# Column sums of an 8192 x 8192 matrix: two rows per partition and load, fp32 sums on TensorE in four column tiles, and a last block in narrowing strips

## The chip, the cores and the metric

The kernel runs on one core of one Trainium2 chip. The metric is the device time of one execution in microseconds (us), lower is better. Profiles show one execution; their span, from the first instruction to the last, is about 1.8 us shorter than the timed figure. "Fast" and "slow" are states of an execution.

## The reference

```python
def setup_inputs():
    return {"x": np.random.randn(8192, 8192).astype(np.float32)}   # seeded

def reference(x):
    return np.sum(x, axis=0)
```

The input is 268.4 MB, the output 32 KB. Every input byte is read once and there is almost no arithmetic per byte.

## The kernel before

It walks over 64 blocks of 128 rows. Each block is a load of 4 MB (a partition gets one row of 32 KB). ScalarE and VectorE cast it to bf16 in four slices, and TensorE sums over the partitions with a column of ones: 16 matmuls of 512 columns. The sums of the left half of the columns stay in PSUM partition 0, those of the right half in partition 64. After the last block two single-partition copies bring them to SBUF, and two stores send them out.

```python
    load_pool = ctx.enter_context(tc.tile_pool(name="loads", bufs=4))
    bf_pool = ctx.enter_context(tc.tile_pool(name="bf", bufs=3))
    ...
    for i in range(n_row_blocks):                      # 64 blocks of 128 rows
        xt = load_pool.tile([P, C], mybir.dt.float32)
        xb = bf_pool.tile([P, C], mybir.dt.bfloat16)
        nc.sync.dma_start(out=xt, in_=xr[i])           # 4 MB
        for s in range(nsplit):                        # 4 casts of 2048 columns
            eng = nc.scalar if s % 2 == 0 else nc.vector
            ...                                        # copy / tensor_copy
        for g in range(n_col_groups):                  # 16 matmuls of 512 columns
            ...                                        # opart = 0 or 64
            nc.tensor.matmul(out=psum[opart:opart + 1, off:off + N], lhsT=ones,
                             rhs=xb[:, g * N:(g + 1) * N],
                             start=(i == 0), stop=(i == n_row_blocks - 1))

    nc.vector.tensor_copy(out=res[0:1, :], in_=psum[0:1, :])
    nc.scalar.copy(out=res[64:65, :], in_=psum[64:65, :])
    nc.sync.dma_start(out=out[0:HALF], in_=res[0:1, :])
    nc.sync.dma_start(out=out[HALF:C], in_=res[64:65, :])
```

## Time and profile before

| | before |
|---|---|
| timed median (three runs; a fourth, below, makes it 646.06) | 645.85 us |
| profiled span | 644.0 us |
| first load landed / last load landed | 13.1 / 626.9 us |
| tail: last landing to the end | 17.1 us |

These are lines of the page of the kernel before: the span, the busy time of each engine with its share of the span, the DMA share (tenths) in 40 slices, the load queue's share of 16 DMA engines, the queue of instruction fetches (packets, MB, share), and the chain of waits that ended last.

```profile
span 644.0 us, 2724 instructions
PE 336.7 (52%) x1024; PEld 97.4 (15%) x1024; DVE 155.6 (24%) x129; ACT 241.6 (38%) x130; POOL 0.3 (0%) x5
DMA  9999999999999999999999999999999999999970
...
q1 hardware_dynamic: 9220, 268.47, 97.0%
q8 instruction: 8, 0.13, 0.1%
...
DMA 88%; ACT 5%; issue 4%; PE 1%; DVE 1%; SPq 0%; ACTq 0%
```

The loads bound the kernel: the 16 DMA engines are busy until the last slice but one, no compute engine is busy for more than about half the span, and the chain is 88% load. To see how fast loads come, look at when VectorE, which waits for each, starts its casts. The next fence is the timeline of VectorE: start, duration, engine, line, operation, count, and in brackets the idle time before it and what ended it.

```profile
568.60 2.36 DVE L52 CAST xb<-xt 128x2048 bf16<-128x2048 f32 x2 [7.35 <-DMA xt<-in_x_dram]
578.31 2.36 DVE L52 CAST xb<-xt 128x2048 bf16<-128x2048 f32 x2 [7.34 <-DMA xt<-in_x_dram]
588.03 2.36 DVE L52 CAST xb<-xt 128x2048 bf16<-128x2048 f32 x2 [7.36 <-DMA xt<-in_x_dram]
```

A 4 MB load lands every 9.71 to 9.72 us, 431.7 GB/s. The end of the chain of waits (start, duration, what) shows the tail, everything after the last landing:

```profile
591.73 35.03 DMA xt<-in_x_dram
626.86 1.91 ACT xb L50
628.81 4.50 PE psum L60 x15
633.34 4.42 DVE res L69
637.78 3.56 ACT res L70
```

A cast, fifteen matmuls, then two PSUM copies that run one after the other although they are on different engines, and 2.7 us of store and end up to 644.0.

### The profile page before, as it was taken

Reading aid. Unit: us, or ns where it says so; the run is one execution under the profiler, and the core shown is the slowest. Engines: PE = TensorE matmul, PEld = TensorE weight load, DVE = VectorE, ACT = ScalarE, POOL = GpSimd, SP = SyncE. Lnnn points to the kernel's source line nnn. Section 1 sums busy time; section 2 is a strip of 40 time slices with the busy share of each in tenths; the row PEclk is TensorE's granted clock in tenths of the full one; section 3 lists DMA queues with packets and bytes.
Section 4 is the critical chain, followed back from the end, with each engine's and each line's share of the span. In section 5 each row is a group of like instructions: output and inputs, shape, how many; then the busy total and the mean of one; then the engine's idle time right before and its main releaser. Section 6 shows DMA issues by size and latency. Waiting matters only on the chain.

```text
span 644.0 us, 2724 instructions
## 1 busy us (share of the span) xinstructions
PE 336.7 (52%) x1024; PEld 97.4 (15%) x1024; DVE 155.6 (24%) x129; ACT 241.6 (38%) x130; POOL 0.3 (0%) x5
## 2 busy tenths in 40 slices
PE   1464653655545644654646546635555547446533
PEld 0111111111111111111111111101111111111110
DVE  1122122222221221221221221221221221222223
ACT  2243243342442442442442432433433433433423
POOL 0000000000000000000000000000000000000000
PEclk9767668667767687678676766676678676876686
DMA  9999999999999999999999999999999999999970
GB/s 387 427 423 440 435 427 423 444 432 426 426 440 434 422 429 442 429 425 433 438 429 427 434 431 432 429 436 434 426 429 430 438 427 430 429 438 429 434 339 2
DMA packets 9233, 268.64 MB, mean 417 GB/s; under 512 B 1026, under 2 KB 1026, under 8 KB 1026
## 3 DMA queue, kind: packets, MB, share of 16 engines
q1 hardware_dynamic: 9220, 268.47, 97.0%
q8 instruction: 8, 0.13, 0.1%
q14 instruction: 5, 0.04, 0.0%
HBM read 268.44 MB, written 0.03 MB: 417 GB/s over the span
## 4 chain that ended last, share of the span: by engine, by line
DMA 88%; ACT 5%; issue 4%; PE 1%; DVE 1%; SPq 0%; ACTq 0%
DMA xt<-in_x_dram 88%; ACT xb L50 5%; PE psum L60 1%; DVE res L69 1%; ACT res L70 1%; SPq L46 0%; ACTq L50 0%
## 5 line engine op out<-in xcount | busy, mean ns | idle before, releaser
L60 PE MATMUL psum<-xb,ones 128*1 128x512 bf16 x1024 | 336.7, 570 | 296.6 <-DVE xb L52 290.7
L50 ACT CAST xb<-xt 128x2048 bf16<-128x2048 f32 x128 | 236.7, 1896 | 391.8 <-DMA xt<-in_x_dram 391.8
L52 DVE CAST xb<-xt 128x2048 bf16<-128x2048 f32 x128 | 151.2, 1224 | 478.0 <-DMA xt<-in_x_dram 478.0
L60 PEld LDWEIGHTS <-ones 128*1 128x1 bf16 x1024 | 97.4, 107 | 535.3 <-issue 521.9
L70 ACT COPY res<-psum 1x4096 f32<-1x4096 f32 x1 | 3.6, 3564 | 7.2 <-DVE res L69 7.2
L69 DVE COPY res<-psum 1x4096 f32<-1x4096 f32 x1 | 4.4, 4411 | 4.1 <-PE psum L60 4.1
L50 ACT ACT_TABLE_LOAD x1 | 1.3, 1283 | 0.7 <-PEq L87 0.7
L37 POOL MEMSET ones<- 128x1 bf16 x1 | 0.1, 102 | 0.3 <-POOLq L87 0.3
L87 POOL MEMSET const-bfloat16-1.0<- 128x1 bf16 x1 | 0.1, 102 | 0.0
L87 POOL MEMSET const-uint8-127<- 128x1 uint8 x1 | 0.1, 102 | 0.0
L87 POOL MEMSET const-float32-0.0<- 128x1 f32 x1 | 0.1, 99 | 0.2 <-issue 0.2
L87 POOL MEMSET const-float32-1.0<- 128x1 f32 x1 | 0.1, 99 | 0.0
## 6 DMA issues: line engine op xcount, KB each, us to landing
xt<-in_x_dram SPq DMA_DIRECT2D x64, 4096.0 KB, 35.0
out_dram<-res SPq DMA_DIRECT2D x2, 16.0 KB
```

The costliest lines, as they stand in the source:

```text
L37: nc.gpsimd.memset(ones, 1.0)
L50: eng.copy(out=xb[:, s * CS:(s + 1) * CS], in_=xt[:, s * CS:(s + 1) * CS])
L52: eng.tensor_copy(out=xb[:, s * CS:(s + 1) * CS], in_=xt[:, s * CS:(s + 1) * CS])
L60: nc.tensor.matmul(out=psum[opart : opart + 1, off : off + N], lhsT=ones, rhs=xb[:, g * N : (g + 1) * N], start=(i == 0), stop=(i == n_row ...
L69: nc.vector.tensor_copy(out=res[0:1, :], in_=psum[0:1, :])
L70: nc.scalar.copy(out=res[64:65, :], in_=psum[64:65, :])
L87: nc = _bacc.Bacc("TRN2", target_bir_lowering=False, num_devices=1)
```

## The change

The intent is to feed the DMA engines larger pieces, to take both casts away (VectorE adds two rows in fp32, TensorE sums in fp32, four matmuls side by side in column tiles of 32), and to shorten the tail: the last block comes in strips of 8, 4, 2, 1 and 1 units of 512 columns, and each strip's sums are copied and stored as soon as they are complete.

```diff
-    xr = x.rearrange("(b p) c -> b p c", p=P)
+    xr = x.rearrange("(b p k) c -> b p k c", p=P, k=K)          # K = 2
-    load_pool = ctx.enter_context(tc.tile_pool(name="loads", bufs=4))
-    bf_pool = ...
+    load_pool = ctx.enter_context(tc.tile_pool(name="loads", bufs=3))
-    ones = const_pool.tile([P, 1], mybir.dt.bfloat16)
+    ones = const_pool.tile([P, 32], F32)
...                                   # casts and bf16 matmuls go
+    for t in range(n_blocks - 1):
+        xt = load_pool.tile([P, K, C], F32, tag="xt")
+        nc.sync.dma_start(out=xt, in_=xr[t])                      # 8 MB
+        for b in range(n_banks):                                  # 4 banks
+            cols = slice(b * BANK, (b + 1) * BANK)                # BANK = 2048
+            nc.vector.tensor_tensor(out=xt[:, 0, cols], in0=xt[:, 0, cols],
+                                    in1=xt[:, 1, cols], op=mybir.AluOpType.add)
+            v = xt[:, 0, cols].rearrange("p (q j i) -> p j q i", q=NQ, j=NJ)
+            for j in range(NJ):              # out=psum[32*j:32*j+32, ...]
+                mm(v[:, j], j, 512 * b, 512, t == 0, False)
...
+    for u0, nu in STRIPS:                    # [(0,8),(8,4),(12,2),(14,1),(15,1)]
+        cols = slice(u0 * 512, (u0 + nu) * 512)
+        nc.sync.dma_start(out=last[:, :, cols], in_=xr[t][:, :, cols])
+    for u0, nu in STRIPS:
...     # add on VectorE where nu >= 4, else both rows go to TensorE; matmuls into psum
+        nc.vector.tensor_copy(out=res[:, 128*u0 : 128*(u0+nu)],
+                              in_=psum[:, 128*u0 : 128*(u0+nu)])
+        nc.sync.dma_start(out=outr[:, u0:u0+nu, :], in_=res[0:97:32, ...])
```

More of the change, by code (lines that the diff above doesn't have):

```diff
@@ L7 @@
 from concourse._compat import with_exitstack
+F32 = mybir.dt.float32
+BANK = 2048
+NQ, NJ, NI = 4, 4, 128
+STRIPS = [(0, 8), (8, 4), (12, 2), (14, 1), (15, 1)]
 @with_exitstack
@@ L19 @@
     R, C = x.shape
-    assert R % P == 0
-    n_row_blocks = R // P
-    N = 512
-    assert C % N == 0
-    n_col_groups = C // N
-    HALF = C // 2
-    xr = x.rearrange("(b p) c -> b p c", p=P)
-    const_pool = ctx.enter_context(tc.tile_pool(name="const", bufs=1))
-    load_pool = ctx.enter_context(tc.tile_pool(name="loads", bufs=4))
-    bf_pool = ctx.enter_context(tc.tile_pool(name="bf", bufs=3))
-    psum_pool = ctx.enter_context(tc.tile_pool(name="psum", bufs=1, space=bass.MemoryType.PSUM))
@@ L34 @@
-    out_pool = ctx.enter_context(tc.tile_pool(name="out", bufs=1))
-    ones = const_pool.tile([P, 1], mybir.dt.bfloat16)
-    nc.gpsimd.memset(ones, 1.0)
-    psum = psum_pool.tile([P, HALF], mybir.dt.float32)
-    nsplit = 4
-    CS = C // nsplit
-    for i in range(n_row_blocks):
-        xt = load_pool.tile([P, C], mybir.dt.float32)
-        xb = bf_pool.tile([P, C], mybir.dt.bfloat16)
-        nc.sync.dma_start(out=xt, in_=xr[i])
-        for s in range(nsplit):
-            eng = nc.scalar if s % 2 == 0 else nc.vector
-            if eng is nc.scalar:
-                eng.copy(out=xb[:, s * CS:(s + 1) * CS], in_=xt[:, s * CS:(s + 1) * CS])
-            else:
-                eng.tensor_copy(out=xb[:, s * CS:(s + 1) * CS], in_=xt[:, s * CS:(s + 1) * CS])
-        for g in range(n_col_groups):
-            if g < n_col_groups // 2:
-                opart = 0
-                off = g * N
-            else:
-                opart = 64
-                off = (g - n_col_groups // 2) * N
-            nc.tensor.matmul(
-                out=psum[opart : opart + 1, off : off + N],
-                lhsT=ones,
-                rhs=xb[:, g * N : (g + 1) * N],
-                start=(i == 0),
-                stop=(i == n_row_blocks - 1),
-            )
@@ L68 @@
-    res = out_pool.tile([P, HALF], mybir.dt.float32)
-    nc.vector.tensor_copy(out=res[0:1, :], in_=psum[0:1, :])
-    nc.scalar.copy(out=res[64:65, :], in_=psum[64:65, :])
-    nc.sync.dma_start(out=out[0:HALF], in_=res[0:1, :])
-    nc.sync.dma_start(out=out[HALF:C], in_=res[64:65, :])
+    K = 2
+    assert R % (P * K) == 0 and C % BANK == 0
+    n_blocks = R // (P * K)
+    n_banks = C // BANK
+    xr = x.rearrange("(b p k) c -> b p k c", p=P, k=K)
+    outr = out.rearrange("(u j i) -> j u i", j=NJ, i=NI)
@@ new lines @@
+    const_pool = ctx.enter_context(tc.tile_pool(name="const", bufs=1))
+    load_pool = ctx.enter_context(tc.tile_pool(name="loads", bufs=3))
+    psum_pool = ctx.enter_context(
+        tc.tile_pool(name="psum", bufs=1, space=bass.MemoryType.PSUM)
+    )
+    res_pool = ctx.enter_context(tc.tile_pool(name="res", bufs=1))
+    ones = const_pool.tile([P, 32], F32)
+    nc.gpsimd.memset(ones, 1.0)
+    psum = psum_pool.tile([P, n_banks * 512], F32)
+    res = res_pool.tile([P, n_banks * 512], F32)
@@ new lines, in mm @@
+    def mm(rhs, j, lo, n, start, stop):
+        nc.tensor.matmul(
+            out=psum[32 * j : 32 * j + 32, lo : lo + n],
+            lhsT=ones,
+            rhs=rhs,
+            start=start,
+            stop=stop,
+            skip_group_check=True,
+        )
+    for t in range(n_blocks - 1):
[3 more added lines that the diff above has]
+            cols = slice(b * BANK, (b + 1) * BANK)
+            nc.vector.tensor_tensor(
+                out=xt[:, 0, cols], in0=xt[:, 0, cols], in1=xt[:, 1, cols],
+                op=mybir.AluOpType.add,
+            )
+            v = xt[:, 0, cols].rearrange("p (q j i) -> p j q i", q=NQ, j=NJ)
+            for j in range(NJ):
+                mm(v[:, j], j, 512 * b, 512, t == 0, False)
@@ new lines @@
+    t = n_blocks - 1
+    last = load_pool.tile([P, K, C], F32, tag="xt")
+    for u0, nu in STRIPS:
+        cols = slice(u0 * 512, (u0 + nu) * 512)
+        nc.sync.dma_start(out=last[:, :, cols], in_=xr[t][:, :, cols])
+    for u0, nu in STRIPS:
+        cols = slice(u0 * 512, (u0 + nu) * 512)
+        for w in range(u0, u0 + nu, 4):
+            m = min(4, u0 + nu - w)
+            rows = [0, 1]
+            if nu >= 4:
+                wc = slice(w * 512, (w + m) * 512)
+                nc.vector.tensor_tensor(
+                    out=last[:, 0, wc], in0=last[:, 0, wc], in1=last[:, 1, wc],
+                    op=mybir.AluOpType.add,
+                )
+                rows = [0]
+            for k in rows:
+                v = last[:, k, w * 512 : (w + m) * 512].rearrange(
+                    "p (q j i) -> p j q i", q=m, j=NJ
+                )
+                for j in range(NJ):
+                    mm(v[:, j], j, 128 * w, 128 * m, False, k == rows[-1])
+        nc.vector.tensor_copy(
+            out=res[:, 128 * u0 : 128 * (u0 + nu)], in_=psum[:, 128 * u0 : 128 * (u0 + nu)]
+        )
+        nc.sync.dma_start(
+            out=outr[:, u0 : u0 + nu, :],
+            in_=res[0 : 97 : 32, 128 * u0 : 128 * (u0 + nu)].rearrange(
+                "j (u i) -> j u i", i=NI
+            ),
+        )
```

## The prediction

> **What bounds it now.** The loads. The queue table gives the load queue 97.0% of the 16 DMA engines' span. PE (52%), ACT (38%) and DVE (24%) are far below; the chain of waits is 88% load. In the timeline 4 MB loads land every 9.71 to 9.72 us (431.7 GB/s), the first at 13.1 us, the last at 626.9. So: 3.4 us of start, 623.5 us of stream (64 x 9.715 = 621.8, rest hiccups), and a tail of 17.1 us from the last landing to the end at 644.0. The tail, from the chain: ACT cast 1.9, fifteen matmuls 4.5, DVE PSUM copy 4.4, then the ACT PSUM copy 3.6, store and end 2.7. Timed median: 645.85.
>
> **What the change does.** It reads the same 268.4 MB. With half as many loads of twice the size, at most a small boundary or descriptor cost goes: 0 to 2.4 us (estimate 1.2). The last block's strips have rows of 16 KB down to 2 KB; I charge 0.5 us.
>
> Removed: all casts (ACT 236.7, DVE 151.2 us busy), off the path but for the last 1.9 us. Added: fp32 adds of 128x2048, four per 19.43 us. The Trainium skill, "VectorE: DVE Perf Modes" (perf-mode tier table), states 2293 ns for an fp32 tensor_tensor of 2048 (the cast here, 1224 ns, agrees with its 1227 for an fp32 copy). So 9.2 us of DVE per 19.43: hidden. PE: 16 fp32 matmuls of 512 columns per 8 MB; "FP8 and Floating Point Precision" (TensorE Precision Notes) states four passes for true fp32. The bf16 ones start about 0.43 us apart at the low clock, and 16 took 5.1 us; four passes make 14 to 27 us per block in series, about a quarter if the four column tiles overlap. Three 8 MB buffers leave two loads queued (39 us) when one lands, so the queue shouldn't starve.
>
> **The tail** is where time changes. Strips land about 9.8, 5.0, 2.5 and 1.25 us before the last one. DVE is in order: block 30's adds occupy it until 10 us before the last landing, so strip 0's adds and copy end about at that landing; then strip 1's add (2.3), its PE work, copy 0.7, then PE work of three small strips. With overlapping column tiles the last PSUM copy ends 6 to 7 us after the last landing; in series 10 to 14. Store and end 2.7 as before. Expected tail 9.5 us, with serial PE up to 16.
>
> **Prediction.** 645.85 - 7.6 (tail) - 1.2 (load boundaries) + 0.5 (narrow strips) - 1 (fewer hiccups, smaller program) = about 636.5 us; 8 in 10 from 631 to 642. Faster by over 2% (below 632.9) 0.19, within 2% 0.77, slower 0.04.
>
> **What would show each step.** Landings 19.4 us apart, 430 to 436 GB/s. DVE adds about 2.3 us each. Strip 1's add, matmuls, three small PSUM copies and a 2.7 us store after the last landing at about 626 us. Starts of the four column tiles within tens of ns if they overlap, a matmul apart if not.
>
> **What would make it wrong.** Larger descriptors lift the stream to 435 GB/s or more. Column tiles in series at the low clock: fp32 PE work exceeds 19.4 us a block, PE bounds, the time rises far above 660. PSUM copies and matmuls of strips sharing a bank wait for each other: 2 to 4 us more. Coarse dependency tracking makes the first strip wait for all five.

## The result, and the profile after

| | before | after |
|---|---|---|
| timed median | 646.06 us | 634.61 us |
| profiled span | 644.0 us | 632.3 us |
| last load landed | 626.9 us | 623.2 us |
| tail | 17.1 us | 9.1 us |

The ratio is 0.9822, 95% interval 0.9808 to 0.9836: 1.8% faster, which counts as the same at a bound of 2%. Ratios here and below are the mean time of one kernel's fast runs over that of the other's fast runs of the same rounds, so not quite the ratio of the medians quoted.

The same lines of the page, now of the kernel after:

```profile
span 632.3 us, 2446 instructions
PE 216.0 (34%) x1064; PEld 25.8 (4%) x1064; DVE 285.4 (45%) x132; POOL 0.3 (0%) x5
DMA  9999999999999999999999999999999999999993
...
q1 hardware_dynamic: 5908, 268.47, 98.2%
q8 instruction: 8, 0.13, 0.1%
...
DMA 81%; DVE 15%; PE 3%; issue 0%; SPq 0%; DVEq 0%
```

ScalarE has dropped out, VectorE works nearly twice as long, and the DMA engines are still the bound. The timeline of VectorE shows the landings of 8 MB loads:

```profile
565.00 8.90 DVE L64 TENSOR_TENSOR xt<-xt 128x2048 f32<-128x2048 f32 x4 [10.39 <-DMA xt<-in_x_dram]
584.31 8.90 DVE L64 TENSOR_TENSOR xt<-xt 128x2048 f32<-128x2048 f32 x4 [10.41 <-DMA xt<-in_x_dram]
```

They are 19.31 us apart (two of before took 19.43), 434.4 GB/s, and VectorE idles for 10.4 us before each. The end of the chain of waits:

```profile
576.64 41.51 DMA last<-in_x_dram
618.18 2.29 DVE last L84
620.47 1.15 DVE res L95
621.66 1.98 PE psum L50 x8
623.66 0.70 DVE res L95
624.40 1.98 PE psum L50 x16
626.40 0.43 DVE res L95
626.88 1.12 PE psum L50 x16
628.03 0.30 DVE res L95
628.38 1.12 PE psum L50 x16
629.52 0.29 DVE res L95
```

From strip 1 on, matmuls (PE) and PSUM copies (DVE res) alternate strictly. The last three strips don't appear as landings: the records of DMA completions show them at 620.6, 621.9 and 623.2, when the work of strip 1 was still under way. So the chain left the loads at 618.2, and each strip's matmuls waited for the copy of the strip before, which reads other columns.

The saving in spans is 644.0 - 632.3 = 11.7 us: 3.6 because the stream of loads ends earlier, 8.1 from the tail. (This is by the completion records, which put the last landing of before at 626.8; the timeline shows a landing about 0.1 us later, when an engine starts on it.)

### The profile page after: what moved, and what is told of

It is laid out like the page before. It is cut to its first block, busy times and chain, and to the rows that moved or that the text cites. A ratio compares the mean times of both kernels' runs of the same rounds, so it can differ in the third digit from the quotient of the medians.

```text
span 632.3 us, 2446 instructions
## 1 busy us (share of the span) xinstructions
PE 216.0 (34%) x1064; PEld 25.8 (4%) x1064; DVE 285.4 (45%) x132; POOL 0.3 (0%) x5
## 3 DMA queue, kind: packets, MB, share of 16 engines
q1 hardware_dynamic: 5908, 268.47, 98.2%
## 4 chain that ended last, share of the span: by engine, by line
DMA 81%; DVE 15%; PE 3%; issue 0%; SPq 0%; DVEq 0%
DMA xt<-in_x_dram 75%; DVE xt L64 14%; DMA last<-in_x_dram 7%; PE psum L50 3%; DVE res L95 0%; DVE last L84 0%; SPq L76 0%; DVEq L64 0%; SPq L61 0%
## 5 line engine op out<-in xcount | busy, mean ns | idle before, releaser
L64 DVE TENSOR_TENSOR xt<-xt 128x2048 f32<-128x2048 f32 x124 | 275.8, 2286 | 336.7 <-DMA xt<-in_x_dram 336.7
L50 PE MATMUL psum<-xt,ones 128*32 128x512 f32 x992 | 206.1, 918 | 407.6 <-DVE xt L64 407.6
L50 PEld LDWEIGHTS psum<-xt,ones 128*32 128x32 f32 x992 | 23.4, 131 | 589.4 <-DVE xt L64 564.5
L50 PE MATMUL psum<-last,ones 128*32 128x128 f32 (+2 forms) x72 | 9.9, 681 | 5.9 <-DVE res L95 3.6
L84 DVE TENSOR_TENSOR last<-last 128x2048 f32<-128x2048 f32 x3 | 6.8, 2289 | 1.1 <-DMA last<-in_x_dram 1.1
L95 DVE COPY res<-psum 128x128 f32<-128x128 f32 (+3 forms) x5 | 2.9, 583 | 6.5 <-PE psum L50 6.5
L50 PEld LDWEIGHTS psum<-last,ones 128*32 128x32 f32 x72 | 2.4, 152 | 13.8 <-DVE res L95 8.4
```

Source lines behind the costliest of these rows:

```text
L50: nc.tensor.matmul(out=psum[32 * j : 32 * j + 32, lo : lo + n], lhsT=ones, rhs=rhs, start=start, stop=stop, skip_group_check=True,)
L64: nc.vector.tensor_tensor(out=xt[:, 0, cols], in0=xt[:, 0, cols], in1=xt[:, 1, cols], op=mybir.AluOpType.add,)
L84: nc.vector.tensor_tensor(out=last[:, 0, wc], in0=last[:, 0, wc], in1=last[:, 1, wc], op=mybir.AluOpType.add,)
L95: nc.vector.tensor_copy(out=res[:, 128 * u0 : 128 * (u0 + nu)], in_=psum[:, 128 * u0 : 128 * (u0 + nu)])
```

## The experiments

Rival theories had to be told apart for each half. For the **stream**: the gain comes from longer rows in each transfer (theory D), from fewer loads (rival L), or from the other compute beside it. For the **tail**: the strips' gain is limited by matmuls that wait for copies they don't need, or by landings and adds. All kernels were run in rounds with the kernel before, whose medians were 645.94, 645.85 and 646.10 us in the three sets. Every result was correct but that of e8, which is wrong on purpose.

| run | time us | ratio to before | last load landed | tail |
|---|---|---|---|---|
| after | 634.61 | 0.9822 | 623.2 | 9.1 |
| e1_rows32k | 635.10 | 0.9830 | 624.4 | 9.1 |
| e2_two_loads | 635.60 | 0.9842 | 624.8 | 9.0 |
| e3_before_big_loads | 643.59 | 0.9969 | 624.4 | 17.2 |
| e4_no_strips | 641.06 | 0.9931 | 623.6 | 16.5 |
| e5_own_banks | 631.29 | 0.9774 | 624.8 | 5.0 |
| e6_tail | 631.65 | 0.9779 | 625.2 | 4.7 |
| e7_dve_casts | 645.89 | 1.0000 | 627.0 | 17.7 |
| e8_no_mid_matmuls | 645.23 | 0.9988 | 625.7 | 17.0 |
| e9_two_buffers | 634.82 | 0.9823 | (profile slow) | |
| e10_five_buffers | 646.21 | 1.0001 | 626.6 | 17.2 |
| e11_serial_tiles | 653.16 | 1.0106 | 623.2 | 26.9 |
| e12_tail_few | 629.83 | 0.9752 | 623.5 | 4.3 |

The last two columns are of the profile: landings are read from the timeline, or from the completion records where nothing waited for them; the tail is the span less that.

### e1: rows of 32 KB in the same loads

```diff
-    xr = x.rearrange("(b p k) c -> b p k c", p=P, k=K)
+    xr = x.rearrange("(b k p) c -> b p k c", p=P, k=K)
```

> The changed kernel, but each partition's two rows lie 128 rows apart in x, so an 8 MB load is made of 256 rows of 32 KB, not 128 of 64 KB; the number of loads, their size and all compute stay. Theory D (a fixed cost per row of the transfer, about 14 ns by the packet durations: 2418 ns for 64 KB against 1216 for 32 KB): an engine's block takes 16 x 1.216 = 19.46 us of packets, so landings are 19.43 to 19.45 us apart, as two loads of the kernel before, and the time is about 634.6 + 31 x 0.125 = 638.4. Rival L (a fixed cost per load, halved by halving their number): landings stay 19.31 us apart and the time stays at 634.6, within 0.5.

It took 635.10 us, 0.5 more than after, where theory D forecast 3.8. The 0.5 is within the noise, as the intervals of the two ratios overlap. In the profiles the last landing is 1.2 us later, but the profiled run of after was the fastest of its four and that of e1 the slowest of its five. The intervals between landings are steadier: blocks land 19.36 us apart (median), 0.05 more than in after, a third to a half of what theory D forecast, and not the standstill of rival L either. The trace's packet records say why the forecast was too large. Medians, in ns:

```
row     2 KB   4 KB   8 KB   16 KB   32 KB                     64 KB
after     84    159    309     611   -                          2418
e1        84    159    309     611   1213                          -
before     -      -      -       -   1213 to 1224, mean 1217       -
```

(The mean leaves out packets of over 1300 ns.) The medians of after and e1 fit, within 1 ns, an estimate worked out from its 84 and 2418 ns: 8.6 ns for each row, and 1 ns for each 27.2 bytes. A row of 64 KB takes 8 ns less than two of 1213 ns, not 14 less than two of 1216. Halving the number of rows saves 8 x 8 ns = 0.06 us per engine and block, as measured. The rest of the stream's gain lies in another column: with the changed compute nearly every 32 KB packet takes 1213 ns (99%), in the kernel before only some (18%).

### e2: two loads of 4 MB for each block

```diff
-        nc.sync.dma_start(out=xt, in_=xr[t])
+        for k in range(K):
+            nc.sync.dma_start(out=xt[:, k, :], in_=xr[t][:, k, :])     # e1's row layout
```

> As e1_rows32k with the same 32 KB rows, but every block comes as two loads of 4 MB. Theory D: nothing is added but one 9 ns packet per engine and load, so landings of a block are 19.43 to 19.46 us apart and the time is that of e1_rows32k within 0.5 us. Rival L: each block gains one more load boundary of about 0.125 us, so 3.9 us more than e1_rows32k.

It took 635.60 us, 0.5 more than e1, and the last load landed 0.4 us later. So 31 more loads cost about 0.5 us, no more than the noise, or some 0.016 us each; rival L, which needed 3.9, falls. With rows and loads as before, the stream of e2 still ends 2.0 us before that of the kernel before: this part belongs to neither theory.

### e3: the large loads alone

```diff
-    load_pool = ctx.enter_context(tc.tile_pool(name="loads", bufs=4))
+    load_pool = ctx.enter_context(tc.tile_pool(name="loads", bufs=2))
-        nc.sync.dma_start(out=xt, in_=xr[i])
+        if k == 0:   # t, k = divmod(i, 2); xr with two rows per partition
+            xk = load_pool.tile([P, K, C], mybir.dt.float32, tag="xt")
+            ...      # one load of 8 MB; the last block as two of 4 MB
+        xt = xk[:, k, :]
```

> The kernel before with its casts, bf16 matmuls and tail, but rows 2p and 2p+1 of a 256-row block in partition p, one load of 8 MB with 64 KB rows, two load buffers; only the last block comes as two loads of 4 MB. If the stream's gain is all the load shape, landings are 19.31 us apart and the time is 646.06 - 31 x 0.125 = 642.2, with a tail of 17.2 us as before. If the gain came from taking away the casts and half of the matmul work (rival), landings stay 19.43 apart and the time stays 646. If two buffers starve the queue, a gap shows before some landings and the time exceeds 646.

It took 643.59 us, 2.4 less than before, with the tail unchanged at 17.2. The load shape alone gives two thirds of the stream's gain here, and less under the changed compute (after against e2: 1.6). The two parts don't add up: 2.4 and 2.0 apart, 3.6 together.

### e7, e8: what stretches the packets of the kernel before?

```diff
# e7
-            eng = nc.scalar if s % 2 == 0 else nc.vector
+            eng = nc.vector
# e8 (wrong result on purpose)
-        for g in range(n_col_groups):
+        for g in range(n_col_groups if i in (0, n_row_blocks - 1) else 0):
```

> The kernel before with all four casts of a block on VectorE, ScalarE idle in the stream. e1 and e2 showed that with the changed kernel's compute a 32 KB packet takes 1213 ns, nearly always; in the kernel before 1213 to 1224, mean 1217 without the slow ones. If ScalarE's writes or reads stretch the packets, they return to 1213 ns here, the loads land 9.67 us apart and the stream is 2 us shorter; the tail gains or loses little (one cast more on VectorE, about 0.5 us). If VectorE's casts or the matmuls do it, the mean stays at 1216 to 1218 and landings at 9.715.

> The kernel before with the matmuls of the first and the last row block only, so with a wrong result on purpose. If TensorE's reads (or its power and clock) stretch the packets, they return to 1213 ns, landings to 9.67 us, and the time falls by 2 us; if the casts do it, the packet mean stays at 1216 to 1218 ns and the time at 646 within 0.6.

Neither found it. With ScalarE idle the packets took the same 1213 to 1224 ns and the time was 645.89. Without the matmuls they did too; the casts alone are not enough either, since in the kernel before the first four loads take 1213 ns and 1217 begins with the sixth, though loads from the second on already stream beside casts. e8 did show something else. Its stream ended 1.2 us earlier (625.7), and this is where, in the timeline of VectorE; first the kernel before, then e8:

```profile
61.73 2.36 DVE L52 CAST xb<-xt 128x2048 bf16<-128x2048 f32 x2 [7.35 <-DMA xt<-in_x_dram]
72.62 2.36 DVE L52 CAST xb<-xt 128x2048 bf16<-128x2048 f32 x2 [8.53 <-DMA xt<-in_x_dram]
```

```profile
61.83 2.36 DVE L52 CAST xb<-xt 128x2048 bf16<-128x2048 f32 x2 [7.35 <-DMA xt<-in_x_dram]
71.55 2.36 DVE L52 CAST xb<-xt 128x2048 bf16<-128x2048 f32 x2 [7.36 <-DMA xt<-in_x_dram]
```

One interval of 10.89 us is back to 9.72. In the kernel before, the DMA records show an instruction fetch of 16 KB at 68 us and seven more later; e8, whose TensorE program is short, has none. The DMA engine that fetches falls about 1.2 us behind, and a load is complete only when the last engine is. The timed gain of e8 was 0.6 us (ratio 0.9988, interval 0.9975 to 1.0000).

### e9, e10: the number of load buffers

```diff
# e9, from after                            # e10, from before
-    ... name="loads", bufs=3               -    ... name="loads", bufs=4   ("bf", bufs=3)
+    ... name="loads", bufs=2               +    ... name="loads", bufs=5   ("bf", bufs=1)
```

> The changed kernel with two load buffers of 8 MB instead of three; nothing else. In the kernel before the first five loads, which meet casts and matmuls already, take 1213 ns a packet, and from the sixth on 1217: from then on each load is issued only when a buffer comes free, with about 3 loads (12 MB) outstanding, and in the changed kernel 16 to 24 MB are. Theory Q (how much is queued behind the running load sets the packet time): here 8 to 16 MB are outstanding, packets go from 2418 to 2420 to 2424 ns as in e3_before_big_loads, landings to 19.35 us, the time to about 635.9. If the depth doesn't matter, packets stay at 2418, landings at 19.31, and the time within 0.5 us of 634.6.

> The kernel before with five load buffers of 4 MB instead of four (and one cast buffer instead of three, for room). Theory Q: with 16 to 20 MB outstanding packets return to 1213 ns, landings to 9.67 us, and the time falls by about 2 us to 643.8. If the depth doesn't matter, the packet mean stays at 1217, landings at 9.715 and the time at 645.9.

Theory Q falls: 634.82 and 646.21 us are the times without the edits, and e10's packets still have a mean of 1217 ns. One of e9's five executions, the profiled one, was slow (763.95 us). In it a 512-column matmul instruction took 2943 ns, 918 in after, TensorE was busy 89% of the span and bounded the kernel. Its trace holds no clock records, so the granted clock of 1.0 that the record gives for it is no reading, and why it was slow stays open. It is left out; e9's packet times can't be compared for this reason. What makes the packets of before 4 ns longer stays open.

### e4: no strips

```diff
-    for t in range(n_blocks - 1):
+    for t in range(n_blocks):
...
-    t = n_blocks - 1                       # and all of the strips
+    nc.vector.tensor_copy(out=res, in_=psum)
+    nc.sync.dma_start(out=outr, in_=res[0:97:32, :].rearrange(...))
```

> The changed kernel without the narrowing strips: the last block is one 8 MB load, summed as the others, then one PSUM copy of 128x2048 and one store. The stream should end about where it does with strips, at 623.0; then four adds 8.9, the last bank's matmuls 1.1 to 1.9, a copy of 2.2, store and end 2.5: a tail of about 15 us (9.1 with strips), span 638.0, time about 640.3. If the strips were worth nothing because matmuls and copies wait for each other, the time stays near 634.6.

It took 641.06 us, 6.5 more than after. Its tail of 16.5 us is nearly that of before (17.1): without strips the new compute would have saved nothing there, because 8 MB are left to add when the last load lands.

### e11: two column tiles, one after the other

```diff
-            for j in range(NJ):
-                mm(v[:, j], j, 512 * b, 512, t == 0, t == n_blocks - 1)
+            for g in range(4 * b, 4 * b + 4):
+                mm(xt[:, 0, 512*g : 512*g + 512], 2 * (g // 8), 512 * (g % 8), 512,
+                   t == 0, t == n_blocks - 1)
...     # the end as in before: two PSUM copies of one partition, two stores
```

> e4_no_strips with two column tiles used one after the other (eight matmuls in the first, then eight in the other, as the kernel before had them), so that no two matmuls in a row are in different tiles but one pair. In the changed kernel eight fp32 passes of four tiles take 1.93 us at the low clock or 1.07 at full clock. If column tiles overlap, four matmuls in a row of one tile take about 4 times as long: 6.8 us at the low clock, 3.4 at full. VectorE delivers a bank every 2.2 us, so TensorE runs on for 14 us or more a block and should reach the full clock: still below 19.3 us a block, the stream is unchanged, and only the tail grows by about 10 us (5 of matmuls, 6 of PSUM copies of one partition) to about 651. If it stays at the low clock, TensorE needs 27 us a block and the time is 850 to 900. If column tiles never overlapped, the matmuls take what they took.

It took 653.16 us, 12.1 more than e4 by the medians. Between the profiles it is 10.0 us, all in the tail (26.9 us against 16.5); the stream ended at 623.2, in e4 at 623.6. About half of that is the matmuls, which end at 639.5 (e4: 634.5); the rest is the PSUM copies of before, 4.4 and 3.6 us one after the other, where e4 has one of 2.3. The timeline of TensorE, e4's last block first (eight instructions are four fp32 matmuls):

```profile
626.00 1.93 PE L50 MATMUL psum<-xt,ones 128*32 128x512 f32 x8 [11.61 <-DVE xt L64]
628.20 1.94 PE L50 MATMUL psum<-xt,ones 128*32 128x512 f32 x8 [0.27 <-DVE xt L64]
```

and e11, a whole block of sixteen matmuls:

```profile
586.91 14.46 PE L49 MATMUL psum<-xt,ones 128*32 128x512 f32 x32 [5.44 <-DVE xt L63]
```

The granted clock is the share of TensorE's full clock that the profile records. In four tiles four matmuls take 1.93 us at a granted clock of 0.50, one after the other 3.6 us on the mean of this block (mean clock 0.84). At equal clocks: in e11 a matmul follows the last after 1.71 us at 0.50 and 0.86 us at 1.0, so four take 6.8 and 3.4 us; in four tiles they take 1.93 and 1.07 (both in the trace of after). Overlap is real, but the stream doesn't need it, as 14.5 us fit under 19.3.

### e5: a PSUM tile for each strip

```diff
-    psum = psum_pool.tile([P, n_banks * 512], F32)
+    psums = [psum_pool.tile([P, max(512, 128 * nu)], F32, name=f"ps{s}")
+             for s, (u0, nu) in enumerate(STRIPS)]
...     # main loop: the matmuls of bank 3 split by strip (256, 128 and 128 columns)
```

> The changed kernel with a PSUM tile, in its own banks, for each strip's sums (before: one PSUM tile for all, the last three strips in one bank); the same strips and adds. In the changed kernel the matmuls of strips 1 to 4 start 0.04 us after the PSUM copy of the strip before, not when their data is there. If those waits cost what the chain of waits shows (copies of 1.15, 0.70, 0.43 and 0.30 us on it, with the hand-overs about 2.9 us), the matmuls now follow one another, the chain holds one 0.29 us copy, the tail falls from 9.1 to about 6.2 us and the time by about 2.9 to 631.7. Rival: the matmuls of the late strips are held by the landings or by the adds, so the copies were not in the way, and the time stays within 0.7 us of 634.6.

It took 631.29 us, 3.3 less than after. The end of its chain of waits:

```profile
577.15 42.34 DMA last<-in_x_dram
619.52 2.30 DVE last L91
621.86 4.72 PE ps L53 x56
626.61 0.29 DVE res L102
```

The 56 instructions of strips 1 to 4 now run in one piece, with one copy behind them. The waits came with the one PSUM tile, not from sums that were needed. The Trainium skill, "PSUM — Partial Sum Buffer" (PSUM bank collisions raise a hardware error), asks for a guard by bank and quadrant; strip 1's bank was never read by the copy it waited for, and e5 runs correctly without that wait. The same holds for strip 2. Strips 2 to 4 share a bank in after, so by that guard strips 3 and 4 have to wait there; e5 gives each strip both its own tile and its own banks, and no run tells the two apart for them.

### e6: finer strips, adds for all but the last, copies on ScalarE

```diff
# against e5
-STRIPS = [(0, 8), (8, 4), (12, 2), (14, 1), (15, 1)]
+STRIPS = [(0, 8), (8, 2), (10, 2), (12, 2), (14, 1), (15, 1)]
-            if nu >= 4:
+            if u0 < 15:
-        nc.vector.tensor_copy(...)
+        copy = nc.vector.tensor_copy if u0 == 15 else nc.scalar.copy
```

> e5_own_banks with the 2048-column strip cut in two, adds of 1024 and 512 columns on VectorE for every strip but the last, and PSUM copies on ScalarE but for the last. By the durations in the profile of the changed kernel (add 2.29 us per 2048 columns, four 512-column matmuls 1.93 us at the low clock) the last strip's matmuls start within 0.3 us of its landing at 623.2 and end 1.1 us later; with a 0.29 us copy and 2.5 us of store and end the span is about 627.4, the tail 4.2 to 4.8 us, the time about 629.5, over 2% below the kernel before. If ScalarE's copies or the one-strip-behind adds hold it up, 630 to 632.

It took 631.65 us: a miss by 2. The tail was 4.7 us, as forecast, but the last load landed at 625.2. In e5 and e6 splitting the matmuls of bank 3 made the TensorE program longer: the records show 12 and 14 fetches of 16 KB within the span, 8 in after (the expectation of e12 counted 13, 15 and 9 with one of another kind). The completion records of the last strip, one for each of 16 DMA engines, fall into groups 1.0 to 1.2 us apart or less:

```
        fetches   engines complete at
after      8      621.6 to 622.6: 8;   623.0 to 623.2: 8
e5        12      621.7 to 622.7: 8;   623.1 to 623.4: 4;   624.4 to 624.8: 4
e6        14      622.0 to 623.0: 8;   623.5: 2;            624.7 to 625.2: 6
```

With 12 fetches four engines are late twice, with 14 six. That the fetches go round eight engines is inferred from these counts; the records don't name the engine.

### e12: the same tail, a short program

```diff
-STRIPS = [(0, 8), (8, 4), (12, 2), (14, 1), (15, 1)]
+STRIPS = [(8, 6), (0, 3), (4, 3), (14, 2), (3, 1), (7, 1)]
-    psum = psum_pool.tile([P, n_banks * 512], F32)
+    psums = [psum_pool.tile([P, 512], F32, name=f"ps{b}") for b in range(n_banks)]
...     # main loop as in after; the strips' adds and copies as in e6
```

> The tail of e6_tail without its longer program: TensorE's main loop is that of the changed kernel (16 matmuls a block, one PSUM tile per bank), and strips are chosen so that neighbours in time are in different banks (columns 8 to 13 of the sixteen 512-column units first, then 0 to 2, 4 to 6, 14 and 15, 3, and 7 last). e5 and e6 fetched 13 and 15 instruction blocks of 16 KB during the stream against 9 in the changed kernel, and show a second block interval lengthened by 1.0 to 1.2 us just after the ninth such fetch (the first after the first fetch). If the ninth fetch hits the DMA engine of the first again, this kernel has one long interval, the last landing at about 623.2, a tail of 4.3 us and a time of 629.3 to 630. If the second long interval is chance, the time is that of e6_tail, 631.5, within 0.6.

It took 629.83 us, ratio 0.9752 (0.9739 to 0.9765): 2.5% below the kernel before and the fastest of all. It has 8 fetches, one long interval (20.66 us, after the first fetch), the last landing at 623.5 and a tail of 4.3 us. After the ninth fetch e5 had an interval of 20.50 us, this kernel 19.29 at the same place; e5 first:

```profile
468.62 8.90 DVE L67 TENSOR_TENSOR xt<-xt 128x2048 f32<-128x2048 f32 x4 [10.40 <-DMA xt<-in_x_dram]
489.12 8.90 DVE L67 TENSOR_TENSOR xt<-xt 128x2048 f32<-128x2048 f32 x4 [11.61 <-DMA xt<-in_x_dram]
```

```profile
468.66 8.90 DVE L64 TENSOR_TENSOR xt<-xt 128x2048 f32<-128x2048 f32 x4 [10.40 <-DMA xt<-in_x_dram]
487.95 8.90 DVE L64 TENSOR_TENSOR xt<-xt 128x2048 f32<-128x2048 f32 x4 [10.39 <-DMA xt<-in_x_dram]
```

## Why the prediction was right or wrong

**The whole: right.** Forecast 636.5 us in 631 to 642, within 2%; measured 634.61.

**What bounds it: right.** DMA engines stay the bound, 98.2% of their span. Adds of 2048 columns took 2286 ns; the Trainium skill's "VectorE: DVE Perf Modes" (the perf-mode tier table) states 2293, and they hide in 19.3 us. e11 shows that even TensorE in series hides.

**The four passes of fp32: right.** "FP8 and Floating Point Precision" (TensorE Precision Notes) states four; in e11 a 512-column matmul takes 0.86 us at the full granted clock, four times the 0.21 to 0.22 us between the bf16 ones of before at that clock.

**The tail: right in size.** Forecast 9.5 us with overlapping tiles, measured 9.1; a last copy 6 to 7 us after the last landing, measured 6.6. The inside was partly different. Strip 1's add went ahead of strip 0's copy, which the forecast had the other way. What was listed as a risk, waits between PSUM copies and matmuls, did happen and costs about 3 us (e5). So that the size came out is partly luck. Strip 0's copy ended at 621.6, 1.6 us before the last landing and not at it, and strip 1's add (2.3 us) no longer stood behind it; these 3.9 us made up for waits that were not in the 9.5. Strips themselves are worth 6.5 us (e4).

**The stream: mis-sized.** The steps "1.2 (load boundaries)" and "1 (fewer hiccups, smaller program)", less 0.5 for narrow strips, summed to 1.7 us; the stream ended 3.6 us earlier. Load boundaries are worth about 0.5 (e2 against e1). Row length is worth about 1.2 by the last landings and 0.5 by the timed medians (after against e1). These parts are rough, as each rests on one profile, and the runs of after alone spread over 0.7 us. The hiccups, instruction fetches, gave nothing: both kernels have eight of 16 KB, and one long interval each (10.89 and 20.83 us, both about 1.2 to 1.5 over the rest). In their place stand some 2 us that the forecast didn't have: packets of 1213 ns in place of 1217 once the compute had changed (e2). What in the compute or the layout does that is not settled: idle ScalarE, absent matmuls and another buffer leave it in place.

## What to carry to other kernels

In this kernel, bound by its loads, about two thirds of the gain lay at the end. In one like it, count the work that stands between the last landing and the last store, and cut the last block so that little of it is left. Then read the chain of waits for waits on things that are not needed, such as one PSUM tile that couples independent strips. Here instruction fetches delayed the DMA engines that carry the data, so a longer program can take back what a shorter tail gives.

## What the Trainium skill lacked or had wrong

- "DMA: Bandwidth & Descriptors" (Bandwidth) lists 16 MB in 79.0 us at 425 GB/s, for DMAs issued from GpSimd; these two figures don't fit each other. Here 8 MB loads, issued from SyncE, land every 19.31 us, 434.4 GB/s, close to the 435.2 of the same page's ceiling.
- The same page has no durations for long rows. Here rows of 2, 16, 32 and 64 KB took 84, 611, 1213 and 2418 ns, so going from 32 to 64 KB saves 8 ns in 2426, and shortened the interval between 8 MB landings by 0.05 us in 19.36 (e1 against after).
- "Runtime: NRT & Kernel Launch" (Instruction fetch mechanics) calls the cost of crossing a 16 KiB boundary of instructions mostly hidden, and gives no cost for loads that run beside it. Here a fetch of 16 KB puts a DMA engine about 1.2 us behind for the rest of the stream, once with 8 fetches and twice for some engines with 12 or 14.
- "TensorE: Matmul & The Clock Gate" (Part 3: Packing small matmuls — row/col tiling) gives 2.38 times for three column tiles and no measured figure for four. Here four fp32 matmuls in four tiles took 1.93 us at half clock and 1.07 at full, against 6.8 and 3.4 in series (e11): 3.5 and 3.2 times.
